# From the gates on: activations stationary, four weight tiles moved in 512-column products (one Trainium2 core)

## The chip, the cores and the metric

One core of a Trainium2 chip runs the whole program. The metric is the device time in microseconds (us), the median of several executions. TensorE (PE) multiplies, VectorE (DVE) and ScalarE (ACT) do the elementwise work, GpSimd (POOL) a little of it, and SyncE (SP) issues nearly all transfers (DMAs).

## What is computed

One layer of a hybrid encoder on 256 tokens of width 2048, in float32:

```python
u   = rmsnorm(h, norm_mix_g)
z   = u @ w_in                      # 2048 x 8704: B_a, C_a, V_a, Q, K, V, gate_a, gate_b
y_a = (b_a * centred_dwconv3(c_a * v_a, conv_a_w)) @ w_out_a        # 1024 x 2048
y_b = windowed_attention(rope(q), rope(k), v, sink) @ w_o_attn      # 1024 x 2048
h   = h + (sigmoid(gl_a + b) * y_a + sigmoid(gl_b + b) * y_b) @ w_mix_out   # 2048 x 2048
up  = centred_dwconv3(rmsnorm(h, norm_ffn_g) @ ffn_w_up, ffn_conv_w) + ffn_conv_b   # 2048 x 11264
h   = h + (silu(up[:, :5632]) * up[:, 5632:]) @ ffn_w_down          # 5632 x 2048
out = rmsnorm(h, norm_final_g)
```

## The kernel before

Everything is kept with features on the 128 partitions and the 256 tokens along the row. A weight matrix lies in memory as tiles of 128 x 128 values. `run(groups)` walks through *chunks* of eight such tiles (512 KB); one chunk is one *step* of the program's schedule. For a chunk, `fetch` issues one transfer on SP into one of five `raw` buffers, `high` (ACT, L176) rounds it to the short format fp32r (`whi`, four buffers), and `low` (DVE, L187) takes the remainder (`wlo`, three buffers). In the program's text `fetch` stands six chunks ahead of the products, `high` three and `low` two. The activations are kept as such a pair too: a row of 512 holds the rounded part of 256 tokens and behind it the remainder.

For each weight tile PE makes a *pair*: the tile's rounded part stands in the array and all 512 activation columns move past it (L215), then its remainder stands and the 256 rounded columns move (L216). Pairs of all k blocks add up in one PSUM bank, features on partitions. `turns` exchanges the two products of a few chosen pairs.

When a tile's last pair is done its *epilogue* begins, a generator that goes on by one `yield` per step: `total` adds the two halves of the bank (ACT copies one half, L245; DVE adds, L249), `scaled` multiplies by the norm's factor (L371), and then comes what the stage wants. The stages in order of time are: key, query, value and convolution columns of `w_in` with the attention between them; 32 tiles of gates; `w_oa` and `w_o` in turn, 16 tiles each with 8 k blocks; `w_mix`, 16 tiles with 16 k blocks; `w_up`, 88 tiles with 16 k blocks (the epilogue `epi_up` does the convolution with L281, L283 and L284, the sigmoid, and the products L669 and L672); `w_dn`, 16 tiles with 44 k blocks, the last of which (`finale`) goes by halves of the tokens. Each queue and engine works in the order in which the program was written. Transfers take eight semaphores in turn, so that an issue waits for the landing of the transfer eight issues earlier.

Of the kernel before, what the change touches and what calls it, by code (L numbers as in the profile page):

```python
# [14 lines left out]
P = 128  # L15
D = 2048
# [10 lines left out]
CH = 8  # L27
WIDE = 6
# [23 lines left out]
def hybrid_block_kernel(ctx: ExitStack, tc: tile.TileContext, head, wide, xT, w_in, w_oa, w_o, w_mix, w_up, w_dn, vec, cst, out):  # L52
# [10 lines left out]
    ct = cpool.tile([P, C_END], F32, tag="ct", name="ct")  # L63
# [3 lines left out]
    ident = ct[:, C_ID : C_ID + P]  # L67
# [62 lines left out]

    def run(groups):

# [17 lines left out]
        def pieces(c):  # L150

            n = len(chunks[c][1])
            return ((0, 2), (2, n)) if c < 3 else ((0, n),)

        def fetch(c):
            w, blocks, pre = chunks[c]
            if pre is not None:
                raws[c] = pre(0, c)
            else:
                raw = wpool.tile([P, CH, P], F32, tag="raw", name="raw", bufs=5)  # L160
                nc.sync.dma_start(raw[:, : len(blocks), :], w)
                raws[c] = lambda a, b, raw=raw: raw[:, a:b, :]


        def high(c):
            _, blocks, pre = chunks[c]
            if pre is not None:
                pre(1, c)
            (_, _, _, _, *halves), k0 = blocks[0]
            if halves:  # L170
                last = lazy("last", lambda: cpool.tile([P, FT, P], F32R, tag="B", name="last"))
                his[c] = last[:, k0 : k0 + len(blocks), :]
            else:
                his[c] = wpool.tile([P, CH, P], F32R, tag="whi", name="whi")
            for a, b in pieces(c):
                nc.scalar.copy(his[c][:, a:b, :], raws[c](a, b))  # L176
            if pre is not None:
                pre(2, c)
# [11 lines left out]
        for c, (_, blocks, _) in enumerate(chunks):  # L190
# [7 lines left out]
            for i, (job, k) in enumerate(blocks):  # L198
                _, n, rhs, epi, *halves = job
# [5 lines left out]
                a, last, half = rhs(k), k == n - 1, bool(halves and k)  # L205
                if order["due"] and n == KT:
# [7 lines left out]
                products = [  # L214
                    lambda: nc.tensor.matmul(both, hi[:, i, :], moving, start=k == 0, stop=last and turned),  # L215
                    lambda: nc.tensor.matmul(  # L216
                        ps[:, 0:T], lo[:, i, :], a[:, 0:T], start=False, stop=last and not turned
                    ),
                ]
# [23 lines left out]
    def total(ps, dst=None):  # L243
        b = spool.tile([P, T], F32, tag="evb", name="evb")
        nc.scalar.copy(b, ps[:, T : 2 * T])  # L245
        yield 1
        if dst is None:
            dst = spool.tile([P, T], F32, tag="evt", name="evt")
        nc.vector.tensor_tensor(dst, ps[:, 0:T], b, op=ALU.add)  # L249
        return dst  # L250

    rr = {}

    def inv_rms(parts, r, tag="tp"):
# [13 lines left out]
        t = spool.tile([P, T], F32, tag="evs", name="nt")[:, 0:n]  # L268
# [19 lines left out]
    def sumsq(k, src, acc):  # L288
        sq = spool.tile([P, T], F32, tag="sq", name="sq") if k else acc
# [65 lines left out]
    def r1():  # L355
# [5 lines left out]
        yield from inv_rms([sq1[:, 0, :]], new_r("r1"))  # L361
# [5 lines left out]
    def scaled(ps, dst=None):  # L367
        t = yield from total(ps)
        if dst is None:
            dst = spool.tile([P, T], F32, tag="evs", name="evs")  # L370
        nc.vector.tensor_tensor(dst, t, rr["r"], op=ALU.mult)  # L371
        return dst
# [228 lines left out]
    def epi_yb(m, ps):  # L601
        gates = box["gates"]
        t = yield from total(ps)
        nc.vector.tensor_tensor(t, t, gates[:, KT + m, :], op=ALU.mult)
# [6 lines left out]
    def epi_mix(m, ps):  # L611
        yield 1
        for i in range(2):
            nc.vector.tensor_tensor(x[:, m, :], x[:, m, :], ps[:, i * T : i * T + T], op=ALU.add)
# [8 lines left out]
    for i in range(2 * KT):  # L623
        groups.append(single(w_in[len(rest) + i], KT, xr, lambda ps, i=i: epi_gate(i, ps)))
    for m in range(KT):
        groups.append(single(w_oa[m], 8, lambda k: box["B"][:, k, :], lambda ps, m=m: epi_ya(m, ps)))
        groups.append(single(w_o[m], 8, lambda k: box["B"][:, 8 + k, :], lambda ps, m=m: epi_yb(m, ps)))

    def outer_first(jobs, n):

        groups.append((4, jobs[:n], None))
        groups.extend((CH, [job], None) for job in jobs[n:])

    outer_first([(w_mix[m], KT, lambda k: merged()[:, k, :], lambda ps, m=m: epi_mix(m, ps)) for m in range(KT)], 3)


    def start_ffn():
# [4 lines left out]
        return actA, actC  # L642
# [7 lines left out]
    def r2():  # L650
        nc.scalar.preload_act_table_set("natural_log_exp_and_others")
        yield from inv_rms([acc2], new_r("r2"))
        later(10, turns)

    def epi_up(i, which, ps):
        c = i + which * FT
        t = yield from scaled(ps)
        yield 1
        lazy("act", start_ffn)
# [10 lines left out]
        else:  # L670
            s = half.pop(i)
# [4 lines left out]
    def epi_dn(m, ps):  # L676
        yield 1
# [4 lines left out]
        for i in range(2):  # L682
            nc.vector.tensor_tensor(h, h, ps[:, i * T : i * T + T], op=ALU.add)
# [3 lines left out]
    def finale(ps):  # L687
# [24 lines left out]
        def norm(half):  # L712

            h = x[:, m, cols(half)]
            sq = spool.tile([P, T], F32, tag="sq", name="sq")[:, 0:H]
            nc.scalar.square(sq, h)
            nc.tensor.matmul(sums[half], ones, sq, start=False, stop=True)  # L717
            ln = spool.tile([P, T], F32, tag="evb", name="ln")[:, 0:H]
            nc.scalar.activation(ln, sums[half], AF.Ln, bias=eps)  # L719
            v = spool.tile([P, T], F32, tag="evt", name="nv")[:, 0:H]  # L720
            nc.vector.tensor_scalar(v, sums[half], EPS, None, op0=ALU.add)
            r0 = spool.tile([P, T], F32, tag="sq", name="r0")[:, 0:H]
            nc.scalar.activation(r0, ln, AF.Exp, scale=-0.5)
            nc.scalar.mul(h, h, col(V_GFIN + m))
            t = spool.tile([P, T], F32, tag="evs", name="nt")[:, 0:H]
# [40 lines left out]
    jobs = []  # L766
    for i in range(FT):
        for which in range(2):
            epi = lambda ps, i=i, which=which: epi_up(i, which, ps)
            jobs.append((w_up[2 * i + which], KT, lambda k: hsplit()[:, k, :], epi))  # L770
    outer_first(jobs, 3)
    jobs = [(w_dn[m], FT, act, lambda ps, m=m: epi_dn(m, ps)) for m in range(KT - 1)]
    outer_first(jobs + [(w_dn[KT - 1], FT, act, finale, True)], 2)
# [23 lines left out]
def _layout(a):  # L797
# [5 lines left out]

    def cols(v):
# [15 lines left out]
    order += range(g0, g0 + 2 * D)  # L820
    up = []
    for i in range(FT):
# [22 lines left out]
        "w_oa": tiles(a["w_out_a"][0]),  # L845
        "w_o": tiles(a["w_o_attn"][0][att, :]),
        "w_mix": tiles(a["w_mix_out"][0]),
        "w_up": tiles(a["ffn_w_up"][0][:, up]),
        "w_dn": tiles(a["ffn_w_down"][0]),
# [23 lines left out]
```

## Time and profile before

| | |
|---|---|
| median of 3 runs | 1331.31 us (1331.3 to 1331.63) |
| profiled execution | 1332.0 us, of which the span of the profile is 1330.2 us |
| instructions | 20480 |
| granted TensorE clock | 0.998 of full speed |
| VectorE, ScalarE, GpSimd busy | 955.7, 723.1, 70.1 us |
| read from memory | 248.16 MB |

The span runs from the first to the last instruction; the profiled execution's own time is 1.8 us longer. Busy times are sums over instructions of one engine, without overlap. An engine off the chain of waits may be idle at no cost.

### The profile page before, as it was taken

Reading aid. Unit: us, or ns where it says so; the run is one execution under the profiler, and the core shown is the slowest. Engines: PE = TensorE matmul, PEld = TensorE weight load, DVE = VectorE, ACT = ScalarE, POOL = GpSimd, SP = SyncE. Lnnn points to the kernel's source line nnn. Section 1 sums busy time; section 2 is a strip of 40 time slices with the busy share of each in tenths; the row PEclk is TensorE's granted clock in tenths of the full one; section 3 lists DMA queues with packets and bytes.
Section 4 is the critical chain, followed back from the end, with each engine's and each line's share of the span. In section 5 each row is a group of like instructions: output and inputs, shape, how many; then the busy total and the mean of one; then the engine's idle time right before and its main releaser. Section 6 shows DMA issues by size and latency. Waiting matters only on the chain.

```text
span 1330.2 us, 20480 instructions
## 1 busy us (share of the span) xinstructions
PE 1320.0 (99%) x7686; PEld 1161.4 (87%) x7686; DVE 955.7 (72%) x1508; ACT 723.1 (54%) x1151; POOL 70.1 (5%) x66
## 2 busy tenths in 40 slices
PE   9999999999999999999999999999999999999997
PEld 8888888888888888888888888888888888888886
DVE  7888777555557887668888888888888865445444
ACT  7667665555555545446555555555555545444442
POOL 0000000000000002430000000000000001111211
PEclk9999999999999999999999999999999999999999
DMA  8786545555555547547555555555555557666663
GB/s 309 234 243 200 199 158 175 182 191 190 191 189 190 190 143 236 188 141 235 190 190 190 191 190 190 190 191 190 191 190 190 174 153 236 194 186 183 197 191 104
DMA packets 76676, 255.54 MB, mean 192 GB/s; under 512 B 8864, under 2 KB 9248, under 8 KB 76576
## 3 DMA queue, kind: packets, MB, share of 16 engines
q1 hardware_dynamic: 76144, 253.44, 59.1%
q8 instruction: 60, 0.98, 0.3%
q10 hardware_dynamic: 432, 0.79, 0.2%
q14 instruction: 40, 0.33, 0.1%
HBM read 248.16 MB, written 2.10 MB: 188 GB/s over the span
## 4 chain that ended last, share of the span: by engine, by line
PE 99%; DVE 0%; ACT 0%; POOLq 0%; issue 0%; DVEq 0%; ACTq 0%
PE ps L215 63%; PE ps L216 33%; PE av L491 1%; PE ptp L478 1%; PE warm L311 0%; PE s L448 0%; PE s L449 0%; PE more L695 0%; POOLq L868 0%; DVE y L737 0%; DVE r L729 0%; DVE x L702 0%; PE nps L259 0%; ACT ln L719 0%; PE nps L717 0%
## 5 line engine op out<-in xcount | busy, mean ns | idle before, releaser
L187 DVE TENSOR_TENSOR wlo<-raw,whi 128x1024 fp32r<-128x1024 f32 (+3 forms) x493 | 568.0, 1154 | 314.4 <-PE ps L216 222.2
L176 ACT CAST whi<-raw 128x1024 fp32r<-128x1024 f32 (+3 forms) x493 | 488.2, 992 | 326.4 <-PE ps L215 187.7
L215 PE MATMUL ps<-hs,whi 128*128 128x512 f32 x1408 | 488.2, 391 | 0.0
L216 PE MATMUL ps<-hs,wlo 128*128 128x256 f32 x1408 | 393.6, 280 | 0.0
L215 PE MATMUL ps<-xs,whi 128*128 128x512 f32 x1088 | 377.4, 392 | 0.0
L215 PEld LDWEIGHTS ps<-hs,whi 128*128 128x128 f32 x1408 | 263.0, 187 | 57.4
L216 PE MATMUL ps<-xs,wlo 128*128 128x256 f32 x1088 | 300.6, 280 | 0.0
L216 PEld LDWEIGHTS ps<-hs,wlo 128*128 128x128 f32 x1408 | 266.1, 189 | 0.4
L215 PEld LDWEIGHTS ps<-xs,whi 128*128 128x128 f32 x1088 | 202.2, 188 | 42.9 <-issue 0.4
L216 PEld LDWEIGHTS ps<-xs,wlo 128*128 128x128 f32 x1088 | 205.8, 189 | 2.4
L245 ACT COPY evb<-ps 128x256 f32<-128x256 f32 x188 | 70.0, 373 | 197.9 <-PE ps L216 194.2
L215 PE MATMUL ps<-actC,whi 128*128 128x512 f32 x420 | 146.2, 391 | 0.0
L216 PE MATMUL ps<-actC,wlo 128*128 128x256 f32 x448 | 124.4, 280 | 0.0
L215 PEld LDWEIGHTS ps<-actC,whi 128*128 128x128 f32 x420 | 78.5, 187 | 17.2
L215 PE MATMUL ps<-ya_att,whi 128*128 128x512 f32 x256 | 88.8, 391 | 0.0
L215 PE MATMUL ps<-ms,whi 128*128 128x512 f32 x256 | 88.8, 391 | 0.0
L216 PEld LDWEIGHTS ps<-actC,wlo 128*128 128x128 f32 x448 | 84.8, 189 | 0.0
L215 PE MATMUL ps<-actA,whi 128*128 128x512 f32 x240 | 83.8, 391 | 0.0
L249 DVE TENSOR_TENSOR evt<-ps,evb 128x256 f32<-128x256 f32 x178 | 74.4, 418 | 0.7 <-ACT evb L245 0.7
L216 PE MATMUL ps<-ya_att,wlo 128*128 128x256 f32 x256 | 71.7, 280 | 0.0
L216 PE MATMUL ps<-ms,wlo 128*128 128x256 f32 x256 | 71.7, 280 | 0.0
L216 PE MATMUL ps<-actA,wlo 128*128 128x256 f32 x256 | 70.9, 280 | 0.0
(144 smaller groups left out, 1050.3 us busy)
## 6 DMA issues: line engine op xcount, KB each, us to landing
raw<-in_w_up_dram SPq DMA_DIRECT2D x170, 512.0 KB, 4.1
raw<-in_w_in_dram SPq DMA_DIRECT2D x124, 512.0 KB, 3.6
raw<-in_w_dn_dram SPq DMA_DIRECT2D x70, 512.0 KB, 4.4
raw<-in_w_mix_dram SPq DMA_DIRECT2D x26, 512.0 KB, 4.3
raw<-in_w_dn_dram SPq DMA_DIRECT2D x36, 256.0 KB, 2.7
raw<-in_w_oa_dram SPq DMA_DIRECT2D x16, 512.0 KB, 3.2
raw<-in_w_o_dram SPq DMA_DIRECT2D x16, 512.0 KB, 3.2
raw<-in_wide_dram SPq DMA_DIRECT2D x14, 512.0 KB, 5.2
```

What stands on the lines that cost most here:

```text
L176: nc.scalar.copy(his[c][:, a:b, :], raws[c](a, b))
L187: nc.vector.tensor_tensor(los[c][:, a:b, :], raw(a, b), his[c][:, a:b, :], op=ALU.subtract)
L215: lambda: nc.tensor.matmul(both, hi[:, i, :], moving, start=k == 0, stop=last and turned),
L216: lambda: nc.tensor.matmul(ps[:, 0:T], lo[:, i, :], a[:, 0:T], start=False, stop=last and not turned),
L245: nc.scalar.copy(b, ps[:, T : 2 * T])
L249: nc.vector.tensor_tensor(dst, ps[:, 0:T], b, op=ALU.add)
L478: nc.tensor.transpose(tp[:, b, n * P : (n + 1) * P], p[:, n, b * P : (b + 1) * P], ident)
L491: nc.tensor.matmul(o[64 * e : 64 * e + 64, 0:T], vtok[:, b, v0 : v0 + HD], pT[e][:, b, :], start=b == 0, stop=b == 1)
```

## The change

From the gates up to three quarters of `w_dn`, four weight tiles that are neighbours go together as a *quad*. The activations stand in the array and the weights move: for each k block and each half of the tokens (128 of them) PE makes three products of 512 columns, the rounded activations with `whi`, their remainder with `whi`, and the rounded ones with `wlo`. A chunk is still 512 KB, two k blocks of one quad. The result of a quad lies in two PSUM banks with tokens on partitions. It is turned back by one DVE transpose of 32 x 32 blocks per bank (into `qd`) and 16 transfers on SP, each of 32 partitions and 1 KB a partition, which put the blocks in their places in `qf`; the weights' columns are stored in an order that makes these runs whole. Four steps after the transfers are issued, the four tiles' epilogues begin: two a step apart, then the last two together. `under_way` lets only one quad at a time (two in the stages up to `w_mix`) be between its transpose and its epilogues. `total` is gone from these epilogues. In `w_mix` and `w_up` the first two quads run side by side, one chunk each in turn. The last four tiles of `w_dn` stay as they were, from a tensor of their own, and `turns` is called when they begin. `ct` and the small evacuation buffers moved into pools that end with the attention.

```diff
+                if kind == ["quad"]:
+                    if k == 0:
+                        banks[id(job)] = quad_banks()
+                        was_quad[0] = True
+                    a, last = rhs(k), k == n - 1
+                    wh, wl = (
+                        w[:, QUAD * i : QUAD * i + QUAD, :].rearrange("p q f -> p (q f)") for w in (hi, lo)
+                    )
+                    for h, ps in enumerate(banks[id(job)]):
+                        ah, al = (a[:, o + h * P : o + h * P + P] for o in (0, T))
+                        nc.tensor.matmul(ps, ah, wh, start=k == 0, stop=False)
+                        nc.tensor.matmul(ps, al, wh, start=False, stop=False)
+                        nc.tensor.matmul(ps, ah, wl, start=False, stop=last)
...
+    def quad(*epis, stage, bufs):
+        def go(banks):
+            while under_way[0] >= bufs:
+                yield 1
+            under_way[0] += 1
+            pool = stage()
+            d = pool.tile([P, 4, 2, QUAD * S], F32, tag="qd", name="qd", bufs=bufs)
+            for h, ps in enumerate(banks):
+                if h:
+                    yield 1
+                nc.vector.transpose(d[:, :, h, :], ps)
+            f = pool.tile([P, 4, 2, QUAD, S], F32, tag="qf", name="qf", bufs=bufs)
+            for a in range(4):
+                for b in range(4):
+                    nc.sync.dma_start(
+                        f[S * b : S * b + S, a].rearrange("p h m i -> p (h m i)"),
+                        d[S * a : S * a + S, b].rearrange("p h x -> p (h x)"),
+                    )
+            for _ in range(4):
+                yield 1
+            for m, epi in enumerate(epis):
+                begin(epi, f[:, :, :, m, :].rearrange("p a h i -> p h a i"))
+                if m < 2:
+                    yield 1
+            under_way[0] -= 1
...
-    def epi_up(i, which, ps):
+    def epi_up(i, which, f):
-        t = yield from scaled(ps)
+        t = scaled_quad(f)
...
+    quads(w_gate, KT, xr, epi_gate, stage1, range(2 * KT))
+    quads(w_oa, 8, lambda k: box["B"][:, k, :], epi_ya, stage1, range(KT))
+    quads(w_o, 8, lambda k: box["B"][:, 8 + k, :], epi_yb, stage1, range(KT))
+    quads(w_mix, KT, lambda k: merged()[:, k, :], epi_mix, stage1, range(KT), side=2)
...
+    quads(w_up, KT, lambda k: hsplit()[:, k, :], lambda t, f: epi_up(*t, f), stage2, up, side=2)
+    quads(w_dn, FT, act, epi_dn, stage2, range(KT - QUAD))
+    for m in range(KT - QUAD, KT - 1):
+        groups.append(single(w_end[m - KT + QUAD], FT, act, lambda ps, m=m: epi_dn(m, ps)))
+    groups.append((CH, [(w_end[QUAD - 1], FT, act, finale, "halves")], None))
```

SP's queue, from `w_mix` into `w_dn`, before (`raw` is a weight buffer):

```order
L161 DMA raw<-in_w_mix_dram 128x512 x12
L161 DMA raw<-in_w_mix_dram 128x1024 x26
L161 DMA raw<-in_w_up_dram 128x512 x12
L161 DMA raw<-in_w_up_dram 128x1024 x170
L161 DMA raw<-in_w_dn_dram 128x512 x22
L161 DMA raw<-in_w_dn_dram 128x1024 x5
```

SP's queue of the changed kernel, from `w_mix` into `w_up`:

```order
L179 DMA raw<-in_w_mix_dram 128x1024 x15
L313 DMA qf<-qd 32x256 x16
L179 DMA raw<-in_w_mix_dram 128x1024
L313 DMA qf<-qd 32x256 x16
L179 DMA raw<-in_w_mix_dram 128x1024 x8
L313 DMA qf<-qd 32x256 x16
L179 DMA raw<-in_w_mix_dram 128x1024
L179 DMA raw<-in_w_up_dram 128x1024 x7
```

The weight transfers, which followed one another, now stand in rows of seven, eight or fifteen with 16 transfers of results between them, and in one place two such sixteens have a single weight transfer between them.

DVE in the middle of `w_up`, before (`up` and `evs` are an epilogue's values, `evt` the sum of a bank's halves):

```order
L669 TENSOR_TENSOR sg<-sg,up_8601 128x256
L283 SCALAR_TENSOR_TENSOR up_8659<-evs,vt,up_8659 128x255
L284 SCALAR_TENSOR_TENSOR up_8659<-evs,vt,up_8659 128x255
L672 TENSOR_TENSOR sg<-sg,up_8659 128x256
L249 TENSOR_TENSOR evt<-ps,evb 128x256
L371 TENSOR_TENSOR evs<-evt,r_6205 128x256
L187 TENSOR_TENSOR wlo<-raw,whi 128x1024 x2
L235 TENSOR_TENSOR actC<-sg,actC 128x256
```

DVE of the changed kernel at the same place (`pq` is a quad's bank; L359 and L360 are the old L283 and L284, L205 is the old L187, L455 the old L371):

```order
L455 TENSOR_TENSOR evs<-qf,r_5878 128x256 x2
L359 SCALAR_TENSOR_TENSOR up_9610<-evs,vt,up_9610 128x255
L360 SCALAR_TENSOR_TENSOR up_9610<-evs,vt,up_9610 128x255
L205 TENSOR_TENSOR wlo<-raw,whi 128x1024
L359 SCALAR_TENSOR_TENSOR up_9636<-evs,vt,up_9636 128x255
L360 SCALAR_TENSOR_TENSOR up_9636<-evs,vt,up_9636 128x255
L309 STREAM_TRANSPOSE qd<-pq 128x4x128
L205 TENSOR_TENSOR wlo<-raw,whi 128x1024
L753 TENSOR_TENSOR sg<-sg,up_9610 128x256
L759 TENSOR_TENSOR sg<-sg,up_9636 128x256
L359 SCALAR_TENSOR_TENSOR up_9660<-evs,vt,up_9660 128x255
L360 SCALAR_TENSOR_TENSOR up_9660<-evs,vt,up_9660 128x255
```

One tile's epilogue stood between two pairs of `low`; now the four epilogues of a quad stand in a cluster, and the next quad's two transposes stand in that cluster, the second one behind most of it.

More of the change, by code (lines that the diff above doesn't have):

```diff
@@ L51, in hybrid_block_kernel @@
 @with_exitstack
-def hybrid_block_kernel(ctx: ExitStack, tc: tile.TileContext, head, wide, xT, w_in, w_oa, w_o, w_mix, w_up, w_dn, vec, cst, out):
+def hybrid_block_kernel(
+    ctx: ExitStack, tc: tile.TileContext, head, wide, xT, w_in, w_gate, w_oa, w_o, w_mix, w_up, w_dn, w_end, vec, cst, out
+):
     nc = tc.nc
@@ L129, in hybrid_block_kernel, with quad_banks @@
     bank_tags = {}
+    taken = [0]
+    def quad_banks():
+        q = taken[0] % 3
+        taken[0] += 1
+        where = [(aps, "s0"), (aps, "s1")], [(aps, "tp2"), (aps, "av")], [(lin, "ps"), (lin, "ps")]
+        return [pool.tile([P, QUAD * P], F32, tag=tag, name="pq") for pool, tag in where[q]]
     def run(groups):
@@ L204, in run @@
                 ps = banks[id(job)]
-                a, last, half = rhs(k), k == n - 1, bool(halves and k)
-                if order["due"] and n == KT:
+                a, last, half = rhs(k), k == n - 1, bool(kind and k)
+                if order["due"] and n >= KT:
                     order["turned"] = {pairs[0] + d for d in order["due"]}
@@ L609, in hybrid_block_kernel, with epi_mix @@
     acc2 = spool.tile([P, T], F32, tag="acc", name="acc2", bufs=1)
[L611 to L614, printed above, removed]
+    def epi_mix(m, f):
+        xm = by_block_of_tokens(x[:, m, :])
+        nc.vector.tensor_tensor(xm, xm, f, op=ALU.add)
         yield 1
@@ L621, in epi_mix, with quads @@
         gsplit_lo(hsplit()[:, m, :], x[:, m, :], col(V_GFFN + m))
[L623 to L634, printed above, removed]
+    def quads(w, n, rhs, epi, stage, tiles, side=1):
+        jobs = []
+        for q in range(len(tiles) // QUAD):
+            four = [lambda f, t=t: epi(t, f) for t in tiles[QUAD * q : QUAD * q + QUAD]]
+            jobs.append((w[q], n, rhs, quad(*four, stage=stage, bufs=2 if stage is stage1 else 1), "quad"))
+        groups.append((2, jobs[:side], None))
+        groups.extend((2, [job], None) for job in jobs[side:])
+    quads(w_gate, KT, xr, epi_gate, stage1, range(2 * KT))
+    quads(w_oa, 8, lambda k: box["B"][:, k, :], epi_ya, stage1, range(KT))
+    quads(w_o, 8, lambda k: box["B"][:, 8 + k, :], epi_yb, stage1, range(KT))
+    quads(w_mix, KT, lambda k: merged()[:, k, :], epi_mix, stage1, range(KT), side=2)
     def start_ffn():
@@ L670, in epi_up @@
         else:
+            while i not in half:
+                yield 1
+            yield 1
             s = half.pop(i)
@@ L681, in epi_dn @@
         h = x[:, m, :]
-        for i in range(2):
-            nc.vector.tensor_tensor(h, h, ps[:, i * T : i * T + T], op=ALU.add)
+        if m < KT - QUAD:
+            h4 = by_block_of_tokens(h)
+            nc.vector.tensor_tensor(h4, h4, ps, op=ALU.add)
+        else:
+            for i in range(2):
+                nc.vector.tensor_tensor(h, h, ps[:, i * T : i * T + T], op=ALU.add)
         sumsq(m, h, box["acc3"])
@@ L764, in finale @@
         scale(1, 12, 16, nc.gpsimd, nc.sync)
[L766 to L773, printed above, removed]
+    up = [(i, which) for i in range(FT) for which in range(2)]
+    quads(w_up, KT, lambda k: hsplit()[:, k, :], lambda t, f: epi_up(*t, f), stage2, up, side=2)
[3 more added lines that the diff above has]
+    groups.append((CH, [(w_end[QUAD - 1], FT, act, finale, "halves")], None))
     run(groups)
@@ L844, in _layout @@
         "w_in": tiles(w[:, order]),
[L845 to L849, printed above, removed]
+        "w_gate": quads(w[:, g0 : g0 + 2 * D]),
+        "w_oa": quads(a["w_out_a"][0]),
+        "w_o": quads(a["w_o_attn"][0][att, :]),
+        "w_mix": quads(a["w_mix_out"][0]),
+        "w_up": quads(a["ffn_w_up"][0][:, up]),
+        "w_dn": quads(a["ffn_w_down"][0][:, : D - QUAD * P]),
+        "w_end": tiles(a["ffn_w_down"][0][:, D - QUAD * P :]),
         "vec": np.ascontiguousarray(vec),
```

106 lines of the change are left out of this document (65 added, 41 removed).

## The prediction

> **What bounds the kernel now.** I read the page's busy times and chain first, then the windows by stage, then the order of starts on PE.
>
> ```profile
> PE 1320.0 (99%) x7686; PEld 1161.4 (87%) x7686; DVE 955.7 (72%) x1508; ACT 723.1 (54%) x1151; POOL 70.1 (5%) x66
> PE 99%; DVE 0%; ACT 0%; POOLq 0%; issue 0%; DVEq 0%; ACTq 0%
> ...
> core 0: us, PE busy (x) PEld busy (x) DVE busy (x) ACT busy (x) POOL busy (x), PEclk, DMA share, GB/s
> 232.00:409.00 177.00, 177.00 (x1022) 155.95 (x1021) 103.61 (x133) 89.52 (x129) 0.00 (x0) 1.00 0.56 188
> 587.00:1075.60 488.60, 488.60 (x2820) 430.72 (x2819) 400.70 (x664) 283.87 (x447) 2.06 (x2) 1.00 0.58 190
> sum 1026.60, PE 1026.60 PEld 905.00 DVE 735.98 ACT 542.18 POOL 57.78; mean PE 205.32 PEld 181.00 DVE 147.20 ACT 108.44 POOL 11.56
> ```
>
> PE is the chain from end to end. The two windows are the gates and `w_up`; the sum row is over five windows that hold just the stages the change touches (from the gates to the twelfth tile of `w_dn`), and PE has no idle time in any of them. DVE is the next engine: in `w_up` it is busy 82% of the time (400.7 of 488.6). The moved work is 512 pairs for the gates, 128 + 128 for `w_oa` and `w_o`, 256 for `w_mix`, 1408 for `w_up`, 12 x 44 = 528 for `w_dn`: 2960 pairs in 1026.6 us, 0.347 us a pair.
>
> **Term 1, the products.** A pair has 768 columns, and a quad has six products of 512 per k block, again 768 a tile: the number of columns stays, the number of products goes from two a tile to one and a half, 4440 in all. What counts is the distance from one 512-column product to the next. The trace has no run of them, so I bound it by the starts (first column).
>
> ```profile
> 240.66 0.63 PE L215 MATMUL ps<-xs,whi 128*128 128x512 f32 x2
> 241.13 0.28 PE L216 MATMUL ps<-xs,wlo 128*128 128x256 f32 x1
> ...
> 600.18 0.39 PE L215 MATMUL ps<-hs,whi 128*128 128x512 f32 x1
> 600.41 0.28 PE L216 MATMUL ps<-hs,wlo 128*128 128x256 f32 x1
> 600.52 0.39 PE L215 MATMUL ps<-hs,whi 128*128 128x512 f32 x1
> ...
> 1309.73 0.28 PE L216 MATMUL ps<-actC,wlo 128*128 128x256 f32 x1
> 1309.85 0.28 PE L215 MATMUL ps<-actC,last 128*128 128x256 f32 x1
> 1309.97 0.28 PE L216 MATMUL ps<-actC,wlo 128*128 128x256 f32 x1
> ```
>
> Where only 256-column products follow one another they are 0.12 apart. A pair of 512 and 256 takes 0.347, so the 256 columns more cost 0.107 and a product of 512 should take 0.12 + 0.107 = 0.227. From below, 512 columns at 0.107 per 256 with nothing between give 0.214; from above, the two 512s that `turns` puts side by side are 0.47 / 2 = 0.235 apart. I take 0.227, worked out from two steady stretches, over 0.235, seen only where the order is disturbed: 4440 x 0.227 = 1007.9, that is 18.7 us less. The ends are 950 and 1043.
>
> By the Trainium skill ("TensorE: Matmul & The Clock Gate", section "Wait — 56ns, not 53.3ns?") products of 512 start 215.7 ns apart; with that the term would be 4440 x 0.2157 = 958 us, 69 less than now. The same rule would give a pair 0.325, and the rows have 0.347, so the trace does not bear it out for these products.
>
> **Term 2, SP's queue.** A quad's result comes back through 16 transfers, all issued on SP, between SBUF and SBUF, 32 partitions each. The nearest rows are the attention's `rot` (32 partitions) and `two` (64), also SBUF to SBUF.
>
> ```profile
> L161 SPq DMA_DIRECT2D raw<-in_w_up_dram x182: 327/328/328, 569.2 to 1054.9; - x182
> L386 SPq DMA_DIRECT2D rot<-qkraw x20: 543/582/615, 44.2 to 93.6; - x20
> L398 SPq DMA_DIRECT2D two<-rcos x20: 462/588/842, 54.6 to 104.6; - x20
> ...
> 68.68 2.45 SPq L386 DMA_DIRECT2D rot<-qkraw  x4
> 71.22 1.00 SPq L161 DMA_DIRECT2D raw<-in_w_in_dram  x2
> ...
> raw<-in_w_up_dram SPq DMA_DIRECT2D x170, 512.0 KB, 4.1
> raw<-in_w_oa_dram SPq DMA_DIRECT2D x16, 512.0 KB, 3.2
> two<-rcos SPq DMA_DIRECT2D x20, 128.0 KB, 2.5
> raw<-in_wide_dram SPq DMA_DIRECT2D x14, 512.0 KB, 5.2
> ```
>
> The first three are issue times on SP (least, median, most, ns): a weight transfer costs SP 328, these small ones 582 and 588. Four `rot` in a row take 2.45 us, 0.61 each, so 16 take 9.8 us, against 0.33 for the transfer they stand in front of. The bounds are 0.50 (between the least rows, 462 and 543; 8.0 us for 16) and 0.61; the shapes are nearest to `rot`, so I take 0.61. SP goes in order: while it issues the 16, no weights are fetched. The last lines are us from issue to landing: 4.1 for the weights of `w_up`, bounded by 3.2 for `w_oa` and 5.2 for the `wide` chunks, and 2.5 for the small `two`, which I take for a result. DMA bandwidth is not the matter: a sixteen moves 0.5 MB, and the engines were 58% busy.
>
> The Trainium skill ("DMA: Bandwidth & Descriptors", section "Issuing engines are not separate DMA queues") calls issue time "usually small relative to the DMA itself", and its table in "Anatomy of one DMA" puts dispatch at about 50 ns. By that 16 issues would take 0.8 us and term 3 would vanish, which is the first rival below; the rows of 582 ns disagree.
>
> **Term 3, the loop through SP and DVE.** Let a quad's last chunk be c. In the program's text its second transpose and its 16 transfers stand in step c+1, before the fetch of c+8, which is the last chunk of the next quad. `low` of c+8 stands on DVE ahead of the next quad's epilogues and of its transposes. So from one second transpose to the next, a loop closes that PE is not in: 16 issues, the landing of c+8, `high`, `low`, and all that stands on DVE up to the next second transpose. Its rows:
>
> ```profile
> L187 DVE TENSOR_TENSOR wlo<-raw,whi 128x1024 fp32r<-128x1024 f32 x417 | 512.5, 1230 | 262.7 <-PE ps L216 180.5 <-issue 76.0 <-ACT whi L176 3.1
> L176 ACT CAST whi<-raw 128x1024 fp32r<-128x1024 f32 x417 | 438.7, 1053 | 277.3 <-PE ps L215 159.2 <-issue 112.0 <-DMA raw<-in_w_mix_dram 1.9
> L371 DVE TENSOR_TENSOR evs<-evt,r 128x256 f32<-128x256 f32 x120 | 51.0, 425 | 4.1
> L283 DVE SCALAR_TENSOR_TENSOR up<-evs,vt,up 128x255 f32<-128x255 f32 x88 | 42.2, 479 | 0.0
> L284 DVE SCALAR_TENSOR_TENSOR up<-evs,vt,up 128x255 f32<-128x255 f32 x88 | 42.6, 484 | 3.1
> L669 DVE TENSOR_TENSOR sg<-sg,up 128x256 f32<-128x256 f32 x44 | 18.5, 420 | 0.0
> L457 DVE TENSOR_REDUCE st<-s 128x2 f32<-128x512 f32 x16 | 11.1, 691 | 0.6
> L292 POOL TENSOR_TENSOR acc<-acc,sq 128x256 f32<-128x256 f32 x29 | 42.5, 1465 | 2.3
> L290 POOL TENSOR_TENSOR sq<-x 128x256 f32<-128x256 f32 x29 | 22.8, 785 | 209.0 <-DVE x L683 166.4 <-DVE x L614 42.5
> ...
> 704.19 1.23 DVE L187 TENSOR_TENSOR wlo<-raw,whi 128x1024 fp32r<-128x1024 f32 x1 [1.14 <-issue]
> 707.84 1.22 DVE L187 TENSOR_TENSOR wlo<-raw,whi 128x1024 fp32r<-128x1024 f32 x1
> ```
>
> The transpose has no row. The nearest is L457, which also reads 128x512 from PSUM: 0.69. I take it; the ends are 0.42 (a 256-column operation) and 1.38 (twice).
>
> In `w_up` the sixteens of SP's queue stand eight weight fetches apart 14 times and, before that, seven apart 7 times (at first `under_way` holds the second quad back and the rest catch up). At eight steps DVE has on the loop 4 `low` (4.92), 3 multiplications by the norm (1.28), 8 of the convolution (3.85), 2 products (0.84) and 2 transposes (1.38): 12.3. The two last rows are 3.65 apart with seven operations of 3.89 between their starts, so durations overlap to 0.94: 11.5. The loop: 9.8 + 4.1 + 1.05 + 11.5 = 26.5 us. PE needs 8 x 12 x 0.227 = 21.8 for that quad: 4.7 too long. At seven steps there are 3 `low`, 4 of the convolution and a remainder of the activations besides, 8.2 in all; the loop is 23.1, PE's part 19.1: 4.0 too long. Together 14 x 4.7 + 7 x 4.0 = 94 us. PE waits for `wlo`, DVE for `whi`, ACT for the transfer, SP for its own queue; the 16 results themselves (9.8 + 2.5 us) are there before the late weights and cost nothing.
>
> **The other stages.** Gates: the epilogue is one multiplication, DVE has 7.1 on the loop, 22.1 against 21.8: 7 x 0.3 = 2 us. `w_oa` and `w_o`: a quad has four chunks, 10.9 us, and SP needs 9.8 + 4 weight issues (the row at 71.22 has two in 1.0, then 0.33 each: 1.6) = 11.4: 8 x 0.5 = 4 us. `w_mix`: the first two quads end together, so 32 transfers stand around one weight fetch; the fetch behind them goes out about 22.6 us after the first bank is full (2.5 + 9.8 + 0.5 + 9.8), its chunk is split at 29 (4.1 + 1.05 + 1.2 later), PE wants it at 21.8: 7 us, once. `w_dn`: 22 chunks a quad; 2.5 + 9.8 + 4.1 + 1.05 + 1.2 = 18.7 is just inside 7 chunks (19.1): nothing. The dropped ACT copies and DVE additions (L245, L249) free engines that wait anyway, nothing. GpSimd's squares in `w_mix` (L290 and L292, 2.3 us a tile) come for two tiles at once, 4.6 against the three steps (8.2) until they are read: nothing. The start and the last four tiles are unchanged.
>
> **Sum.** The profiled execution took 1332.0 (span 1330.2; the median of the runs is 0.7 lower): 1332.0 - 18.7 + 94 + 2 + 4 + 7 = 1420.
>
> Its own range: with 0.50 per issue, weights landing in 3.2 and transposes of 0.42 the loops are 23.3 and 20.0, the stalls 20 + 6 + 3 for the rest, 1342. With landing at 5.2, transposes of 1.38 and products of 0.235 in the stages that PE still bounds (2328 x 0.008 = 19) the loops are 28.9 and 25.5, the stalls 99 + 45 + 15, in all 1491.
>
> **Rivals.** (a) Faster: the issues are cheap. The loop at eight steps is 16.7 us beside the issues, so below (21.8 - 16.7) / 16 = 0.32 us each PE bounds `w_up`; at the weights' own 0.33 the stalls are about 0 to 6, and the time is 1332 - 18.7 + 0 to 6, some 1313 to 1320. For it: 1 KB a partition is half of `rot`'s. Against it: `two`, with twice the partitions of `rot`, cost the same, so size is not what sets it. 15%. (b) The change doesn't shorten the products: at 0.235 nothing is gained on PE, the stages outside `w_up` give 19 back, 1439. For it the rows at 240.66, against it the steady stretches. 10%. (c) DVE is what bounds: transposes of 1.38 lengthen every loop by 1.3, 1420 + 21 x 1.3 = 1447; nothing in the trace shows this operation. 10%. The likeliest, the loop near its central price, has 60%; 5% is left for a loop partly covered, 1325 to 1342.
>
> The likeliest with (b) and (c), which only add to it, holds 80%, 1342 to 1491. The range reaches down to the edge of (a), whose rest it leaves out with the very top, some 15% together: 1318 to 1485. A measurement of this kernel can tell about 0.2% (2.7 us) from no change: faster 0.15, same 0.03, slower 0.82.
>
> **What the changed profile would show.** PE busy falls from 99% to about 92%, with waits of `wlo` products in `w_up`, ACT's `whi` and DVE's `wlo` waiting for the transfers of `in_w_up` (now a few us in all); SP busy about 9.8 us in one piece per quad, issues of `qf` near 0.6; distance of products 0.227 within a chunk; gates and `w_dn` about as long as before or shorter, `w_up` near 575 us instead of 488.6. It is wrong if `qf` is issued in 0.3 us, if products of 512 run at 0.214, or if fetches turn out not to stand behind the sixteens.

## The result and the profile after

The changed kernel takes 1466.72 us (median of 4 runs, 1464.72 to 1470.75) against 1331.3 us: 1.1021 times as long, 95% interval 1.0995 to 1.1046. Slower was forecast, at 1420 us in a range of 1318 to 1485. The profiled execution took 1468.0 us, its span 1466.2. The page first: the busy times, and the chain by engine and by line.

```profile
PE 1362.8 (93%) x6206; PEld 1108.7 (76%) x6206; DVE 933.0 (64%) x1390; ACT 668.8 (46%) x971; POOL 55.8 (4%) x66
PE 43%; SPq 26%; DMA 13%; DVE 9%; issue 4%; ACT 3%; POOL 1%; DVEq 0%; POOLq 0%; ACTq 0%
```

PE was 99% of the chain and is 43%; SP's queue now has 26% and the transfers 13%. DVE and ACT are less busy than before: no engine is short of time, they wait for one another. The windows by stage show where. First three of the kernel before that were not shown yet (`w_oa` with `w_o`, `w_mix`, twelve tiles of `w_dn`), then the changed kernel: gates, `w_oa` with `w_o`, `w_mix`, `w_up`, `w_dn`, last four tiles.

```profile
409.30:498.10 88.80, 88.80 (x514) 78.30 (x513) 73.04 (x125) 46.00 (x80) 0.00 (x0) 1.00 0.52 174
498.10:586.80 88.70, 88.70 (x514) 78.20 (x513) 62.38 (x87) 41.69 (x55) 31.12 (x29) 1.00 0.57 189
1075.50:1258.50 183.00, 183.00 (x1058) 161.35 (x1057) 96.14 (x114) 81.10 (x98) 24.60 (x21) 1.00 0.67 197
```

```profile
232.00:410.00 178.00, 175.96 (x769) 143.63 (x768) 95.64 (x113) 76.61 (x93) 0.00 (x0) 1.00 0.58 203
410.00:521.00 111.00, 94.92 (x385) 73.83 (x385) 62.04 (x89) 38.28 (x47) 0.00 (x0) 0.96 0.54 181
521.00:633.00 112.00, 97.05 (x385) 75.91 (x384) 66.63 (x90) 40.97 (x53) 16.95 (x21) 0.91 0.54 183
633.00:1206.00 573.00, 517.99 (x2117) 410.44 (x2115) 386.02 (x603) 253.94 (x349) 10.02 (x11) 0.95 0.52 182
1206.00:1391.00 185.00, 182.25 (x794) 148.70 (x793) 100.20 (x111) 77.63 (x88) 12.85 (x15) 1.00 0.62 196
1391.00:1466.00 75.00, 64.07 (x404) 57.05 (x402) 38.33 (x57) 25.20 (x36) 15.73 (x16) 0.96 0.46 151
```

`w_up` lost 84 us, and the two short stages 22 and 24, a quarter of their length each. The column behind the last engine's busy time is the granted clock: 1.00 everywhere before, 0.91 to 0.96 where PE waits now.

The prices asked for in the prediction: starts of 512-column products in the gates; issues of `qf` on SP (least, median, most, ns); the transpose (busy us, mean ns); us to landing.

```profile
240.03 0.39 PE L228 MATMUL pq<-whi,xs 128*128 128x512 f32 x1
240.26 0.39 PE L229 MATMUL pq<-whi,xs 128*128 128x512 f32 x1
240.49 0.39 PE L230 MATMUL pq<-wlo,xs 128*128 128x512 f32 x1
```

```profile
L313 SPq DMA_DIRECT2D qf<-qd x720: 507/589/1910, 255.8 to 1403.7; - x180
...
L309 DVE STREAM_TRANSPOSE qd<-pq 128x512 f32<-128x512 f32 x90 | 63.6, 708 | 5.3 <-PE pq L230 5.3
...
raw<-in_w_up_dram SPq DMA_DIRECT2D x176, 512.0 KB, 4.5
qf<-qd SPq DMA_DIRECT2D x720, 32.0 KB, 1.8
```

Products are 0.227 apart (median of all gaps). Sixteen issues in a row take 10.0 us in `w_up`. The prices taken were 0.227, 9.8, 0.69, 4.1 for the weights' landing and 2.5 for the results'; measured are 0.227, 10.0, 0.71, 4.5 and 1.8. Now one turn of the loop in `w_up`, from one second transpose to the next, in the order of time.

```profile
971.32 0.71 DVE L309 STREAM_TRANSPOSE qd<-pq 128x512 f32<-128x512 f32 x1
972.05 10.01 SPq L313 DMA_DIRECT2D qf<-qd  x16
982.17 10.78 SPq L179 DMA_DIRECT2D raw<-in_w_up_dram  x8
983.39 0.43 DVE L455 TENSOR_TENSOR evs<-qf,r 128x256 f32<-128x256 f32 x1 [4.73 <-DMA qf<-qd]
986.06 1.04 ACT L194 CAST whi<-raw 128x1024 fp32r<-128x1024 f32 x1 [10.22 <-DMA raw<-in_w_up_dram]
987.14 1.23 DVE L205 TENSOR_TENSOR wlo<-raw,whi 128x1024 fp32r<-128x1024 f32 x1 [3.32 <-ACT whi L194]
997.78 0.71 DVE L309 STREAM_TRANSPOSE qd<-pq 128x512 f32<-128x512 f32 x1
```

The first weight goes out at 982.17, behind the sixteen. ACT stood still 10.2 us for it, then DVE 3.3 us for ACT. From transpose to transpose it is 26.46 us. The fourth row is a wait that the prediction had put at nothing: DVE also stood 4.73 us for the results `qf`. Here that wait ends 3.7 us before the other. The page of waits (us in total, times, longest) has both:

```profile
ACT whi L194 <- DMA raw<-in_w_up_dram: 215.0, 41, 11.3
DVE wlo L205 <- ACT whi L194: 150.8, 55, 3.5
DVE evs L455 <- DMA qf<-qd: 114.7, 30, 6.3
```

### The profile page after: what moved, and what is told of

Same layout as the page of the kernel before. It is cut to its first block, busy times and chain, and to the rows that moved or that the text cites. A ratio compares the mean times of both kernels' runs of the same rounds, so it can differ in the third digit from the quotient of the medians.

```text
span 1466.2 us, 18128 instructions
## 1 busy us (share of the span) xinstructions
PE 1362.8 (93%) x6206; PEld 1108.7 (76%) x6206; DVE 933.0 (64%) x1390; ACT 668.8 (46%) x971; POOL 55.8 (4%) x66
## 4 chain that ended last, share of the span: by engine, by line
PE 43%; SPq 26%; DMA 13%; DVE 9%; issue 4%; ACT 3%; POOL 1%; DVEq 0%; POOLq 0%; ACTq 0%
SPq L313 25%; PE ps L252 10%; PE pq L230 9%; PE pq L228 8%; PE pq L229 8%; DMA raw<-in_w_up_dram 6%; PE ps L253 6%; DVE wlo L205 5%; ACT whi L194 2%; DMA raw<-in_w_o_dram 2%; DVE qd L309 2%; DMA raw<-in_w_gate_dram 1%; DMA raw<-in_w_mix_dram 1%; DMA raw<-in_w_oa_dram 1%; DVE up L359 1%
## 5 line engine op out<-in xcount | busy, mean ns | idle before, releaser
L205 DVE TENSOR_TENSOR wlo<-raw,whi 128x1024 fp32r<-128x1024 f32 (+3 forms) x465 | 557.9, 1208 | 307.0 <-ACT whi L194 150.8
L228 PE MATMUL pq<-whi,hs 128*128 128x512 f32 x704 | 286.9, 408 | 44.0 <-ACT whi L194 44.0
L230 PE MATMUL pq<-wlo,hs 128*128 128x512 f32 x704 | 287.0, 408 | 11.0 <-DVE wlo L205 10.9
L229 PE MATMUL pq<-whi,hs 128*128 128x512 f32 x704 | 282.9, 402 | 0.0
L252 PE MATMUL ps<-xs,whi 128*128 128x512 f32 x576 | 200.2, 394 | 0.0
L228 PEld LDWEIGHTS pq<-whi,hs 128*128 128x128 f32 x704 | 137.8, 196 | 80.4 <-ACT whi L194 52.8
L230 PEld LDWEIGHTS pq<-wlo,hs 128*128 128x128 f32 x704 | 137.9, 196 | 52.5 <-DVE wlo L205 23.7
L229 PEld LDWEIGHTS pq<-whi,hs 128*128 128x128 f32 x704 | 138.4, 197 | 29.5
L253 PE MATMUL ps<-xs,wlo 128*128 128x256 f32 x576 | 158.1, 280 | 0.0
L455 DVE TENSOR_TENSOR evs<-qf,r 128x256 f32<-128x256 f32 x120 | 47.9, 419 | 114.7 <-DMA qf<-qd 114.7
L253 PEld LDWEIGHTS ps<-xs,wlo 128*128 128x128 f32 x576 | 108.8, 189 | 1.9
L230 PE MATMUL pq<-wlo,xs 128*128 128x512 f32 x256 | 100.2, 391 | 1.2 <-DVE wlo L205 1.0
L228 PE MATMUL pq<-whi,xs 128*128 128x512 f32 x256 | 99.9, 390 | 0.8 <-ACT whi L194 0.8
L229 PE MATMUL pq<-whi,xs 128*128 128x512 f32 x256 | 99.7, 389 | 0.0
L229 PE MATMUL pq<-whi,actC 128*128 128x512 f32 x168 | 65.4, 389 | 0.0
L228 PE MATMUL pq<-whi,actC 128*128 128x512 f32 x168 | 65.4, 389 | 0.0
```

Source lines behind the costliest of these rows:

```text
L205: nc.vector.tensor_tensor(los[c][:, a:b, :], raw(a, b), his[c][:, a:b, :], op=ALU.subtract)
L228: nc.tensor.matmul(ps, ah, wh, start=k == 0, stop=False)
L229: nc.tensor.matmul(ps, al, wh, start=False, stop=False)
L230: nc.tensor.matmul(ps, ah, wl, start=False, stop=last)
L253: lambda: nc.tensor.matmul(ps[:, 0:T], lo[:, i, :], a[:, 0:T], start=False, stop=last and not turned),
L455: nc.vector.tensor_tensor(by_block_of_tokens(dst), f, by_block_of_tokens(rr["r"]), op=ALU.mult)
```

## The experiments

The question was which wait holds the quads apart, and what becomes of the time when it is gone. All versions are edits of the changed kernel's `quad()` or of its weight fetch. Lengths of the stages, from a stage's first product to the next stage's, in us; the last column is the median time of the runs:

| kernel | gates | `w_oa`,`w_o` | `w_mix` | `w_up` | `w_dn`, 12 tiles | whole |
|---|---|---|---|---|---|---|
| before | 177.7 | 88.7 | 88.7 | 488.6 | 183.0 | 1331.3 |
| changed | 178.1 | 111.2 | 112.4 | 572.6 | 185.0 | 1466.7 |
| spread over steps, five steps | 174.3 | 92.9 | 103.7 | 482.8 | 179.5 | 1337.9 |
| weights on GpSimd's queue | 174.3 | 112.0 | 109.0 | 544.9 | 181.5 | 1441.7 |
| sixteen on GpSimd's queue | 174.3 | 106.1 | 105.7 | 523.5 | 181.5 | 1405.0 |
| 32 transfers of half the size | 248.7 | 180.2 | 160.4 | 782.3 | 218.0 | 1907.8 |
| five steps, in one piece | 179.3 | 112.4 | 112.7 | 523.9 | 184.8 | 1421.2 |
| weights on GpSimd, five steps | 174.3 | 87.0 | 94.9 | 485.3 | 179.5 | 1338.7 |
| spread, SP and ACT, five steps | 174.3 | 87.0 | 93.2 | 479.2 | 179.5 | 1318.0 |
| spread, SP and GpSimd, five steps | 174.3 | 87.0 | 89.2 | 479.2 | 179.5 | 1321.3 |
| spread, four steps | 174.3 | 112.9 | 112.7 | 552.0 | 186.6 | 1444.0 |
| halves on SP and ACT, four steps | 174.3 | 99.5 | 104.5 | 509.8 | 181.0 | 1372.9 |

**The price of an issue.**

```
-                    nc.sync.dma_start(f[S*b : S*b+S, a] ..., d[S*a : S*a+S, b] ...)
+                    for h in range(2):
+                        nc.sync.dma_start(f[S*b : S*b+S, a, h] ..., d[S*a : S*a+S, b, h])
```

> Each of the sixteen transfers in two of half the bytes (16 KB, 512 B per partition), 32 issues per quad on SP, at the same place. Theory (a price per issue of 0.59 us, whatever its bytes): each quad's loop grows by 9.4 to 9.8 us; 45 quads, of which the four in w_dn and the last have slack: about 1467 + 40 x 9.6 = 1850 (1790 to 1910), and w_up's quads stand 36 us apart. Rival (bytes set the price): 0.3 us each, the whole within 1% of 1467. Rival 2 (SP's queue isn't what bounds): the whole within 3% of 1467.

It took 1907.75 us, 1.4327 times before (1.4299 to 1.4356). The row of the issues (ns) in this version:

```profile
L314 SPq DMA_DIRECT2D qf<-qd x1440: 507/588/1733, 253.5 to 1842.6; - x180
```

Half the bytes, the same 588 ns. The 720 issues more cost 441 us, 0.61 each, and `w_up`'s quads stand 36 us apart; the whole is at the upper end of the expected range. An issue has the same price for 32 and for 16 KB, and the rest waits for SP's queue: both rivals fall.

**The place of the transfers.** Four per step over four steps, so that weight fetches stand between them, then one step more.

```
             for a in range(4):
                 for b in range(4):
                     nc.sync.dma_start(...)
+                yield 1
-            for _ in range(4):
-                yield 1
+            yield 1
```

> The same 720 transfers, four per step over four steps instead of sixteen in one step, so that weight fetches stand between them on SP; the one step's delay that this adds is taken from the four waiting steps (five in all instead of four). Theory (the loop through SP's queue): a fetch waits for at most four issues (2.4 us) instead of sixteen (9.4 to 9.8), the loop in w_up falls from 26.5 to about 19, under PE's 21.8, so w_up is bound by PE at about 480 us instead of 573; w_oa and w_o, where SP is full whatever the order, stay near 105 to 111; w_mix falls to about 95 to 100; the whole about 1345 to 1365. Rival 1 (DVE's transposes and epilogues make the loop, or the slower clock does): w_up keeps 560 to 575, the whole within 1% of 1467. Rival 2 (the transfers' traffic slows the weights' landing, wherever they stand): the same, no gain.

1337.86 us (1.0048 of before, 1.0033 to 1.0063), a little under the expectation: the same transfers on the same queue, and 129 of the 135 us are gone. `w_up` is as expected. `w_oa` with `w_o` took 92.9 us where 105 to 111 were expected, so SP's queue doesn't hold these stages up whatever the order, and `w_mix` took 103.7 against 95 to 100. The windows of `w_oa` with `w_o`, `w_mix` and `w_up`:

```profile
405.40:498.30 92.90, 89.49 (x385) 72.93 (x384) 55.94 (x76) 35.98 (x41) 0.00 (x0) 0.98 0.67 199
498.30:602.00 103.70, 93.26 (x385) 75.18 (x384) 67.92 (x95) 41.84 (x53) 14.16 (x15) 0.95 0.62 193
602.00:1084.90 482.90, 480.46 (x2116) 396.59 (x2115) 386.12 (x591) 259.34 (x347) 16.69 (x16) 1.00 0.67 218
```

PE is busy through `w_up`, and DVE is no less busy there than in the changed kernel (386.1 against 386.0 us). So neither DVE's work nor the load of the DMA engines was the bound, but the order. The edit has two parts, though, place and step; the next ones part them.

**The weights on another queue.**

```
-                nc.sync.dma_start(raw[:, : w.shape[1], :], w)
+                nc.gpsimd.dma_start(raw[:, : w.shape[1], :], w)
```

> The sixteens stay in one piece on SP, and the weights' transfers are issued by GpSimd's queue instead. Theory (order on SP's queue): no fetch stands behind a sixteen; w_up about 480 us, w_oa and w_o about 92 (SP needs 9.8 of the 10.9 us per quad), w_mix about 92, the whole about 1320 to 1345 if GpSimd issues a weight transfer in under 2.7 us (one step) and its squares in w_mix don't hold it up. Rival 1 (DVE or the clock makes the loop): within 1% of 1467. Rival 2: GpSimd's issue is dear (over 2.7 us), then the weights are late everywhere and the whole is above 1467. Rival 3: transfers of 32 KB between partitions and weights compete in the DMA engines, so that the loop keeps part of its length: 1380 to 1467.

1441.66 us, 1.0833 of before (1.0815 to 1.0851): a miss. No weight stands behind a sixteen any more, and only 25 us come back (11 are lost at the start, which is longer with the weights on this queue). DVE's rows in `w_up` say why:

```profile
1028.96 0.42 DVE L455 TENSOR_TENSOR evs<-qf,r 128x256 f32<-128x256 f32 x1 [6.73 <-DMA qf<-qd]
1029.30 1.22 DVE L205 TENSOR_TENSOR wlo<-raw,whi 128x1024 fp32r<-128x1024 f32 x1
```

The epilogue stands on DVE four steps behind the transfers, 10.9 us of PE's time; the last result lands 13.7 us after the second transpose (mean of 13 quads). DVE waits in order, and the next `wlo`, whose weights have long been there, waits behind it. From transpose to transpose it is 24.9 us (the same 13). That is a second loop, through the results, beside the one through the weights. The time also lies in the range of rival 3, which has a share in it: with the weights' transfers beside them, results land 4.3 us after their issue instead of 1.8 (medians), and the last one lands 1.5 us later than in the changed kernel. It is no more than a share: with this queue and the step together (below) the landing is as slow, 4.1 us, and `w_up` takes 485 us.

**The step alone, and step and queue together.**

```
-            for _ in range(4):
+            for _ in range(5):
```

> The changed kernel with five steps instead of four between a quad's transfers and its first epilogue; the sixteen stay in one piece on SP, the weights behind them. It is the control for the spread version, which also has five steps, and tells apart two waits that run side by side in w_up: SP's sixteen hold back the weights (whi and wlo late), and DVE stands before its first epilogue until the last of the sixteen has landed. Theory A (the weights come last: in the trace at 983 to 987 us DVE's epilogue is released at 983.4, the late wlo starts at 987.1): nothing changes, w_up 560 to 575, the whole 1450 to 1475. Theory B (DVE's wait for the results makes the loop): w_up falls by 21 x 2.4 = 50 us or more, the whole about 1410.

> As the version with the weights on GpSimd's queue, and five steps instead of four before the first epilogue. There w_up fell only from 573 to 545 us, quads 24.5 apart; DVE stood 6.7 us in one place for the results. Theory (two waits in parallel, the weights behind the sixteen and DVE behind the results; each hides the other): with both taken away w_up is bound by PE, 478 to 490 us, the whole 1350 to 1380 (w_oa, w_o and w_mix keep about 100 to 110 each, SP's queue being full there). Rival (GpSimd's issue of the weights or the DMA engines' load is what is left): w_up stays near 545, the whole near 1440.

With both taken away: 1338.69 us (1.0051 of before, 1.0037 to 1.0065), better than expected, `w_up` 485.3, and `w_oa` with `w_o` 87.0, PE's own time. With the step alone: 1421.19 us (1.0671, 1.0656 to 1.0686), near theory B's number, but the trace has A's loop. DVE waits for no `evs` any more; its wait is again the weights:

```profile
962.26 1.23 DVE L205 TENSOR_TENSOR wlo<-raw,whi 128x1024 fp32r<-128x1024 f32 x1 [6.88 <-ACT whi L194]
...
969.99 0.71 DVE L309 STREAM_TRANSPOSE qd<-pq 128x512 f32<-128x512 f32 x1
```

The loop has got shorter. Its four parts in us, means over the changed kernel's 14 turns of eight steps and over the last 13 turns with five steps, which also have eight (transpose and issues; landing of the first weight; until its `wlo` starts; until the next second transpose):

| | turns | issues | landing | to `wlo` | to transpose | period |
|---|---|---|---|---|---|---|
| changed | 14 | 10.92 | 3.90 | 1.17 | 10.65 | 26.64 |
| five steps | 13 | 11.12 | 3.91 | 1.16 | 7.74 | 23.93 |

All of the gain is in the last part: a step later, three of the old quad's four pairs of convolution operations (L359, L360) and two products stand behind the new quad's second transpose; in the changed kernel they stand ahead of it. Theory A was right about the loop and wrong that nothing would change.

**Place without the step.**

```
             for a in range(4):
                 for b in range(4):
                     nc.sync.dma_start(...)
+                yield 1
-            for _ in range(4):
-                yield 1
```

> The spread version (four transfers per step) without its fifth step: the first epilogue follows in the fourth step, as in the changed kernel. It parts the two edits of the spread version, the place of the transfers and the step. Theory (two loops side by side): the loop through the weights is gone (a fetch waits for four issues), the loop through the results stays, since the last transfer is issued about 11.6 us after the second transpose, lands 1.3 to 2.7 later, and DVE stands before its epilogue; w_up's quads 24 to 25 us apart (24.5 with the weights on GpSimd's queue and four steps), w_up 535 to 560, w_oa and w_o 105 to 115, the whole 1400 to 1450. Rival (the place of the transfers is all that matters): as the spread version, w_up near 483, the whole 1335 to 1345.

1443.99 us (1.0846, 1.083 to 1.0862), as the theory of two loops says, the rival is 100 us off. The total of DVE's waits for results, 114.7 in the changed kernel, is here:

```profile
DVE evs L453 <- DMA qf<-qd: 177.7, 30, 8.7
```

So either loop alone keeps `w_up` at 524 to 552 us and `w_oa` with `w_o` at 112 to 113; only with both gone is PE the bound.

**Other queues for the transfers.** All on GpSimd's queue; every second one on ACT's, in one piece (`[b % 2]`); every second one on ACT's or GpSimd's, spread, with five steps.

```
-                    nc.sync.dma_start(
+                    nc.gpsimd.dma_start(                           # all
+                    (nc.sync, nc.scalar)[b % 2].dma_start(         # halves; spread with ACT
+                    (nc.sync, nc.gpsimd)[b % 2].dma_start(         # spread with GpSimd
```

> The sixteens in one piece, issued by GpSimd's queue instead of SP's. Theory (order on SP's queue): SP has only the weights, the loop is gone; how long the quad's results take is set by GpSimd's issue, which no trace of this case shows yet. At up to 0.6 us each (9.6 per quad, under the 10.9 us that PE has for a quad in w_oa and w_o) the whole is 1313 to 1340; above 0.68 us w_oa and w_o lengthen in proportion, above 1.36 us (21.8 / 16) w_up is bound by GpSimd's queue and the whole is above 1467. Rival (DVE or the clock makes the loop): within 1% of 1467 at cheap issues.

1405.01 us (1.055, 1.0534 to 1.0565), a miss for the same reason as with the weights there. GpSimd issues in 496 ns, but the row breaks off, most often after ten:

```profile
1027.88 4.88 POOL L313 DMA_DIRECT2D qf<-qd  x10 [14.29 <-DVE qd L309]
1033.29 0.98 POOL L313 DMA_DIRECT2D qf<-qd  x2 [0.53 <-DMA qf<-qd]
1034.90 2.01 POOL L313 DMA_DIRECT2D qf<-qd  x4 [0.62 <-DMA qf<-qd]
```

In 87 of its 93 stops within a sixteen the next issue starts 0.28 us after the landing of the transfer eight issues earlier. That is the program's own wait, since transfers take eight semaphores in turn. So a sixteen still takes about 9 us, and a result lands 4.1 us after its issue (median); DVE waits 5 to 8 us a quad for them in the later part of `w_up`.

> The changed kernel with every second of the sixteen issued on ACT's queue, in one piece and with four steps: only the time of a sixteen is halved, to about 5.2 us. Theory (both loops are shorter by the 5.4 us): in w_up the loop through the weights falls from 26.4 to 21.0 and the one through the results from 24.5 to 19, both under PE's 21.8, so w_up is 479 to 486; w_oa and w_o 87 to 90 (the serial loop 13.8 to 15 there falls to 8 to 9.5, under 10.9), w_mix 91 to 98; the whole 1316 to 1330. Rival (eight issues in a row on ACT hold up whi, or the results' landing is set by the DMA engines, not by the issues): 1335 to 1400.

1372.9 us (1.0306, 1.0289 to 1.0324): the rival. Halving the sixteen shortens both loops, and a third stands up. ACT issues eight transfers ahead of the next `high`:

```profile
961.35 0.71 DVE L309 STREAM_TRANSPOSE qd<-pq 128x512 f32<-128x512 f32 x1
962.09 5.30 ACTq L313 DMA_DIRECT2D qf<-qd  x8
967.49 1.05 ACT L194 CAST whi<-raw 128x1024 fp32r<-128x1024 f32 x1 [9.13 <-DMA qf<-qd]
968.57 1.23 DVE L205 TENSOR_TENSOR wlo<-raw,whi 128x1024 fp32r<-128x1024 f32 x1 [5.40 <-ACT whi L194]
```

7.2 us from transpose to `wlo` and 15.9 of DVE's work until the next second transpose at 984.46 make 23.1, and PE needs 21.8.

> The spread version with every second transfer issued on ACT's queue, the others on SP's: 8 issues per quad and queue. In the spread version only w_oa, w_o and w_mix are longer than PE needs (92.9 and 103.7 us, PE's products 86 or so in each), where SP's 9.8 + 4 x 0.53 = 11.9 us a quad stand against PE's 10.9. Theory (SP's occupancy): SP has 7.0 a quad, w_oa with w_o and w_mix fall to 86 to 90 each, the rest stays, the whole 1336 - 5 to 7 - 14 to 17 = 1313 to 1320, below the kernel before by about 1%. Rival (ACT's issues, 8 x 0.6 = 4.8 us per quad in front of whi, make the weights late): 1325 to 1350.

> The spread version with every second transfer issued on GpSimd's queue (0.49 us each where all stood there), the others on SP's. Theory (SP's occupancy): as with ACT's queue, w_oa with w_o and w_mix 86 to 90 each, the whole 1313 to 1320. Rival (GpSimd's transfers wait for earlier ones in one piece, as after ten of them in the version with all sixteen on it, and its squares in w_mix stand in the way): w_mix stays at 95 to 104, the whole 1322 to 1337.

With ACT 1318.01 us, 0.9898 of before (0.9883 to 0.9913); with GpSimd 1321.28 us, 0.9922 (0.991 to 0.9935). Both are faster than the changed kernel, and by 1.0 and 0.8% than the kernel before. The chain with ACT, and its windows of `w_mix` and `w_up`:

```profile
PE 96%; DVE 1%; DMA 1%; issue 0%; ACT 0%; ACTq 0%; SPq 0%; POOLq 0%; DVEq 0%
...
492.40:585.60 93.20, 89.39 (x386) 72.99 (x385) 66.82 (x89) 42.46 (x54) 16.95 (x18) 0.98 0.68 210
585.60:1064.80 479.20, 479.20 (x2116) 396.89 (x2115) 385.13 (x588) 251.34 (x341) 13.92 (x14) 1.00 0.70 218
```

PE is the chain again, with the shorter products. `w_mix`, expected at 86 to 90 us, keeps 6 us of stalls, where two quads end together. With GpSimd `w_mix` is 4 us shorter still, but the span ends 16.2 us after the last `w_end` product instead of 9.2. The version with all sixteen on GpSimd's queue ends in the same way, and none without results on that queue does. Why is open, since the profile has no work in that stretch, only the closing semaphores.

## Why the prediction was right in sign and 47 us short

- **Term 1, products.** Right: 0.227. Where PE is the bound again, the stages are shorter by what the term said: with ACT's queue gates, `w_oa` with `w_o`, `w_up` and `w_dn` are 3.4, 1.7, 9.4 and 3.5 us under before; their shares of the 18.7 are 3.2, 1.6, 8.9 and 3.3. Rival (b) is out.
- **Term 2, an issue on SP.** Right: 10.0 us for sixteen against 9.8, 0.61 an issue in the doubled version. Rival (a), cheap issues, is out. The Trainium skill ("DMA: Bandwidth & Descriptors", section "Anatomy of one DMA") gives its 50 ns for the dispatch of a transfer that GpSimd issues. They are no price for a whole issue here: one takes 496 ns on GpSimd's queue and 513 to 606 on SP's and ACT's (medians).
- **Term 3, the loop in `w_up`.** 572.6 us against 575; the period 26.6 against 26.5 (its parts 10.9, 3.9, 1.2 and 10.6 against 9.8, 4.1, 1.05 and 11.5, so small errors cancelled), in the seven-step stretch 22.0 to 23.9 against 23.1. DVE's transpose is 0.71, so rival (c) is out.
- **The step that failed** is the sentence in term 3 that "the 16 results themselves (9.8 + 2.5 us) are there before the late weights and cost nothing". It holds in `w_up` as long as the weights are later, and it named that cover. It was carried into `w_oa` and `w_o`, where only SP's occupancy was summed, 11.4 us a quad. There a quad has four chunks, so the four steps end just where the next quad's second transpose stands:

```profile
454.66 12.39 SPq L313 DMA_DIRECT2D qf<-qd  x16
467.14 1.95 SPq L179 DMA_DIRECT2D raw<-in_w_o_dram  x4
468.61 0.42 DVE L679 TENSOR_TENSOR gates<-gates,qf 128x256 f32<-128x256 f32 x1 [4.67 <-DMA qf<-qd]
468.95 0.71 DVE L309 STREAM_TRANSPOSE qd<-pq 128x512 f32<-128x512 f32 x1
469.69 12.51 SPq L313 DMA_DIRECT2D qf<-qd  x16
```

  Sixteen, landing, epilogue, second transpose, next sixteen: nothing overlaps, 15.0 us here, 12.6 to 15.2 over the quads, against PE's 10.9. Beside it SP is full for as long: with the step added, which takes DVE's wait out, SP still needs 12.50 + 1.95 a quad and the stage stays at 112.4; with the weights elsewhere and no step, 112.0; with both, 87.0. The term was 4 us of stalls and measured 24 (111.2 less the 87.0 of PE's own time).
- **Mis-sized on the way:** a sixteen in `w_oa` takes 11.4 to 12.5 us, not 9.8, with four weight transfers issued just ahead of it; with the weights on GpSimd's queue it takes 10.1 to 10.6 there. The trace shows the cause. In the sixteens of `w_oa` and `w_o` one to three of the sixth to eighth issues come late, by up to 1.4 us, and each of these 16 starts 16 or 17 ns after the landing of the weight transfer eight issues earlier, whose semaphore it takes.
- **`w_mix`:** 7 us were forecast for two sixteens around one fetch, and that one stall is 7.3. The stage lost 24: it begins with SP behind by what `w_o` left, and at its other quads PE stalls too, by 0.9 to 3.5 us from start to start.
- **The clock,** not in the prediction at all. After some stalls products start 0.43 apart instead of 0.23 for 3.4 us:

```profile
963.01 0.63 PE L229 MATMUL pq<-whi,hs 128*128 128x512 f32 x1
963.43 0.63 PE L230 MATMUL pq<-wlo,hs 128*128 128x512 f32 x1
...
966.42 0.39 PE L230 MATMUL pq<-wlo,hs 128*128 128x512 f32 x1
966.64 0.39 PE L228 MATMUL pq<-whi,hs 128*128 128x512 f32 x1
```

  In `w_oa`, `w_o` and `w_mix` 66 gaps of 0.3 to 0.45 are about 11 us longer than at full rate (26.3 measured less 66 x 0.227). How much of that the stages are longer by isn't shown. In `w_up` 153 such gaps cost nothing: DVE stands idle for PE before a transpose only once there (0.76 us), and the period is the sum of its other parts. In `w_oa` and `w_o` it does so only once as well.
- **`w_dn` and the end,** forecast unchanged, lost 2.0 and 3.6 against before, 5.3 and 3.6 against forecast. `w_dn` was "just inside" with 18.7 of 19.1 us, and a sixteen of 10.6 used the margin up (stalls of 1.9, 0.9 and 0.9 us from start to start). The last quad's sixteen lies ahead of `w_end`'s weights (1393 to 1404), and PE stops four times, 4.0 us in all, soon after.

By stages, from the gates to the end, the differences to the forecast are 1.6 + 20.1 + 18.3 - 1.1 + 5.3 + 3.6 = 48 us (the profiled execution's 1468 less 1420): the large term was right, the 47 of the median are the small ones. That the time lies in the range is in part luck. The range left at most 15 us for stalls outside `w_up`, and there were 56, counted by stage against the version spread over SP and ACT; the room came from the 144 us that the upper end gave `w_up`, of which 93 were needed.

## What to carry to other kernels

When a step puts a block of slow issues into a queue, write down every engine that stands in order behind them: here the weights behind the issues and the epilogue behind the results were two loops of nearly one length, so that removing one gave 23 to 46 us and removing both 128 or 129 of the 135. A wait costed at nothing because another is later must be priced again in each stage, and again for every repair. Spreading the same transfers over the steps in which their results aren't yet needed, and over two queues, was worth 149 us here, with no operation made faster.

## What was not expected of the hardware

- An issue between two parts of SBUF costs 0.61 to 0.63 us in a row whether it moves 32 or 16 KB; with two at a time and the rest between, the median on SP is 513 ns, and GpSimd's queue takes 496. With eight semaphores in turn a row of sixteen also waits for landings: 0.28 us after the landing on GpSimd's queue, 16 or 17 ns after it on SP's, the next issue starts.
- The clock: in ten traces (all but the doubled version's and the one before) none of 83 isolated stalls of PE of 0.7 to 2.35 us was followed by half rate, and 28 of 42 longer ones were (from start to start, with no other stall within 3 us). The Trainium skill ("TensorE: Matmul & The Clock Gate", section "What's actually happening") puts the idle clock after a window of about 3.4 us; here it comes from 2.35 us on, and not always.
